# Conditioning products in longer runs, and layer 1's conditioning weights in half-size tiles that lie in the places of the partial sums

## The chip, the cores and the metric

The kernel runs on one core of a Trainium2 chip. The metric is the device time of one execution in microseconds (us), and the figure compared is the median of the runs.

## What is computed

Two transformer layers over 256 image tokens `x` and 256 context tokens `ctx`, each of width 2048. Layer 0 mixes by sliding-window attention (16 query heads, 4 key heads), layer 1 by latent attention (16 heads). Both are wrapped alike:

```
for i in range(2):
    shift, scale, gate = split(silu(c) @ ada_w[i] + ada_b[i], 3)      # the same for c_ctx
    h = rmsnorm(x, norm_g[i]) * (1 + scale) + shift                   # and hc from ctx
    o, oc = mixer_i(h, hc)                                            # projections, attention, gate, output product
    x = x + gate * o                                                  # and ctx in layer 0
```

The change touches the products `silu(c) @ ada_w[i]` for shift and scale. There are two rows (the vector `c` and the vector `c_ctx`) against a matrix of 2048 by 4096 for each layer. The gate third of `ada_w` is computed elsewhere, on VectorE, and is not touched.

## The kernel before, in words

**Wide and narrow products.** Nearly all of TensorE's work is wide: `mm3` makes a float32 product out of three fp32r products of 128 rows by 128 columns of weights, with 512 or 256 columns moving. Each weight tile of 128 x 1024 lands in a place named `raw`, ScalarE rounds it into `whi`, VectorE subtracts to get `wlo` (two places each), and TensorE uses both. The conditioning products are narrow: `sil` holds silu of both vectors, padded to 32 columns, so one product `mm_ada` uses 32 of the array's 128 columns (`tile_position=(0, 32 * j)`), in plain float32, and four of them stand side by side for j = 0 to 3. Their weights move through and need no split. A group of narrow products that is to stay together is written inside `with together(340.0)`, where 340 is what the planner adds in nanoseconds for such a group.

**Layer 0's narrow products** (`ada_first_tasks`) come in nine batches (`BATCHES`) of 1, 2 or 4 blocks of 128 outputs for shift and as many for scale. Their weights are loaded as 128 tiles of 128 x 512 (256 KB) into eight places named `k`, up to `AHEAD_K` ahead. A batch of 1 or 2 blocks cuts a tile into four pieces of 128 columns, and a batch of 4 blocks into two of 256. The products are issued as soon as four pieces are there: with every tile, or with every second one.

**Layer 1's narrow products** (`ada_rest_tasks`) are four parts of 16 tiles of 128 x 1024 (512 KB) each. Each tile lands in one of the four `raw` places, which it shares with the wide weights, and brings four products of 256 columns. They are mixed (`merge`) among the 16 gate tasks of layer 0, whose weights are `wgate`.

**Partial sums.** `atile` gives a tile of 128 x 512 in one of 24 places named `acc`. Through the input projection all 24 hold partial sums. In the last of the five groups of the projection, 16 of them are written out to DRAM (`spill`) and read back later piece by piece (`kn`, `acc`). After that the places are taken one by one by the 16 gate tiles `sg`.

**What sets the order.** Python code walks the tasks (`queue`, `step`, `pump`) and only records operations. Then `settle` replays them with a table of costs: at each turn it takes the engine that is free first and gives it the ready operation with the earliest due time. Places of a pool are given out strictly in the order in which tiles were recorded. A load is issued by SyncE (SP) as soon as its place is free and its turn has come; SP's queue is one line, so a load that waits for its place holds up those behind it. `ahead` decides how far loads and splits are recorded ahead of their use. The planner reckons a load at 2000 ns and 320 bytes a nanosecond. TensorE, too, runs its instructions strictly in the order settled here.

Of the kernel before, what the change touches and what calls it, by code (L numbers as in the profile page):

```python
# [11 lines left out]
F32 = mybir.dt.float32  # L12
# [21 lines left out]
SIDE = [0.85, 0.9, 0.8, 0.95, 1.0]  # L34
AHEAD_DMA, AHEAD_SPLIT, AHEAD_K = 0, 1, 6
LAT_T1, LAT_M1, LAT_ADA = 6.072, 6.867, 1.15
# [111 lines left out]
class Node:  # L148
    __slots__ = ("eng", "emit", "occ", "lat", "key", "n", "deps", "outs", "left", "ready", "start",
                 "end", "news", "tiles", "alt", "need", "order")  # L150

    def __init__(self, eng, emit, occ, lat, key, n):
        self.eng, self.emit, self.occ, self.lat, self.key, self.n = eng, emit, occ, lat, key, n
        self.deps, self.order, self.outs, self.news = [], [], [], []
        self.ready, self.start, self.end, self.alt = 0.0, None, None, None


SEM = 100.0
DMA_LAT, DMA_RATE = 2000.0, 320.0


class Plan:
# [57 lines left out]

    def group(self, eng, calls, occ, lat):

        real = {"PE": self.nc.tensor}[eng]
        outs, ins = [], []
        for op, args, kw in calls:
            outs.append(args[0])
            ins += [x for x in list(args[1:]) + list(kw.values()) if isinstance(x, View)]

        def emit():
            for op, args, kw in calls:  # L230
                getattr(real, op)(*[x.real() if isinstance(x, View) else x for x in args],  # L231
                                  **{n: x.real() if isinstance(x, View) else x for n, x in kw.items()})
        self.node(eng, emit, occ, lat, outs, ins)

    def node(self, eng, emit, occ, lat, outs, ins):
# [62 lines left out]
    def settle(self):  # L298
# [52 lines left out]
        for v in nodes:  # L351
            if not v.left:
                offer(v)
        out = []
        while len(out) < len(nodes):
            best = None
# [13 lines left out]
            while waiting[e] and waiting[e][0][0] <= at:  # L370
                _, _, v = heapq.heappop(waiting[e])
                heapq.heappush(able[e], (v.key, v.n, v))
            _, _, v = heapq.heappop(able[e])
            v.start = at
# [69 lines left out]
def tile_hybrid_two_layer(ctx: ExitStack, tc: tile.TileContext, a: dict):  # L444
# [71 lines left out]
    class together:  # L516


        def __init__(self, extra=0.0):
            self.extra = extra  # L520

# [3 lines left out]
        def __exit__(self, *x):  # L525
            calls = run.pop()
            occ = self.extra + sum(c[3] for c in calls)
            plan.group("PE", [c[:3] for c in calls], occ, occ + 165.0)

    def mm(ps, l, r, start, stop, share=1, **k):  # L530
        n = 1
        for d in r.shape[1:]:
            n *= d
        occ = (4 * n / 2.4 / share + (0 if share > 1 else 10) if l.dtype == F32 else max(54.0, 0.428 * n + 10))
        c = ("matmul", (ps,), dict(lhsT=l, rhs=r, start=start, stop=stop, **k), occ)
        if run:
            run[-1].append(c)
        else:
            plan.group("PE", [c[:3]], occ, occ + 165.0)
        clock[0] += (n / 2400.0 + 0.003) * (4 if l.dtype == F32 else 1) / share  # L540
# [41 lines left out]
    def ahead():  # L582
        i = head[0]
        wk = {"w": AHEAD_DMA if i >= FIRST else -1, "k": AHEAD_K}
        n = {"w": 0, "k": 0}
        for j in range(i, min(len(queue), i + 40)):
            t = queue[j]
            if t["src"] is None:
                continue
            kind = t.get("kind", "w")  # L590
            if "raw" not in t and n[kind] <= wk[kind]:
                if kind == "w":
                    t["raw"] = wp.tile([P, 1024], F32, tag="raw", name=nm("raw"))
                else:
                    t["raw"] = ktile(F32)
                SP.dma_start(t["raw"][:, :t["n"]], t["src"])
            n[kind] += 1
        n = 0
        for j in range(i, min(len(queue), i + 40)):
            t = queue[j]  # L600
            if t["src"] is None or not t["split"]:
                continue
# [139 lines left out]
    def ada_first_tasks(bi):  # L742
# [7 lines left out]
        def gen(q):  # L750
            def g(w):
# [5 lines left out]
                box["w"] += [(q * r + u, w[:, u * n:(u + 1) * n]) for u in range(r)]  # L757
                if len(box["w"]) < 4:
                    return
                with together(340.0):  # L760
                    for i, wu in box["w"]:
                        ck, j = divmod(i, ng)
                        mm_ada(box["ps"], ck, j + ng * (ck % half), wu, n, half)
# [17 lines left out]
    def ada_rest_tasks(sec, hf):  # L781
# [3 lines left out]

        def gen(ck):
            def g(w):
                if ck == 0:
                    box["ps"] = mmps()
                with together(340.0):  # L790
                    for j in range(4):
                        mm_ada(box["ps"], ck, j, w[:, j * 256:(j + 1) * 256], 256)
                yield
            return g

        for ck in range(KT):
            out.append(dict(src=a["ada1"][sec, hf, ck], n=1024, gen=gen(ck), split=False, key=None))

# [962 lines left out]
def _layout(i):  # L1761
# [22 lines left out]
    o["crow"] = C(np.concatenate([i["c"][0], i["c_ctx"]]).reshape(8, 512))  # L1784
    o["ada1"] = C(rest.reshape(2, KT, P, 2, 1024).transpose(0, 3, 1, 2, 4))

# [61 lines left out]
```

## Time and profile before

| | before |
|---|---|
| median of 3 runs (lowest to highest) | 1282.94 us (1281.44 to 1283.48) |
| the profiled execution, its time | 1277.38 us |
| its span (first to last instruction) | 1275.6 us |
| TensorE busy (PE) | 1228.1 us, 96% |
| VectorE / ScalarE busy | 930.9 us, 73% / 596.1 us, 47% |
| records of TensorE | 8252, of which 1408 belong to narrow products (two records each) |

Reading: the profiled execution is 5.6 us below the median, so a sum made against it is carried over to the median by ratio. PE counts matmuls whose ends are modelled, so starts are the better thing to measure by. "issue" in brackets is idle time in which the engine waited for nothing that the profile shows.

### The profile page before, as it was taken

The page shows a single profiled execution, that of the slowest core. Times are in us where ns is not written, and L with a number is a line of the kernel's source. Part 1 is how long each engine was busy: PE and PEld are TensorE (multiplying, and loading weights), DVE is VectorE, ACT ScalarE, POOL GpSimd, SP SyncE. Part 2 cuts the span into 40 slices and gives each one's busy share as a digit, 9 for nine tenths or more (in the row PEclk, how much of TensorE's full clock was granted, in tenths as well). Part 3 has the DMA queues.
Part 4 walks back from the last instruction along what each step waited for, and adds up shares of the span by engine and source line. Part 5 has one row for each costly group of instructions (what it writes and reads, how often), then busy time and mean ns, then how long its engine had stood idle before and what let it go on. Part 6 is the DMA issues. An engine that isn't in the chain of part 4 may idle for free.

```text
span 1275.6 us, 22429 instructions
## 1 busy us (share of the span) xinstructions
PE 1228.1 (96%) x8252; PEld 1046.5 (82%) x8252; DVE 930.9 (73%) x2260; ACT 596.1 (47%) x1434; POOL 79.7 (6%) x105
## 2 busy tenths in 40 slices
PE   3999999999999999999999999997999999999998
PEld 2777776778777777777789888986999999999998
DVE  5567687899737667667788766985588888888554
ACT  4623212222235445445565322553567777776432
POOL 0000000000100101000000000000111111110000
PEclk9999999999999999999999999998999999999999
DMA  9876797557855455455537877762343333332664
GB/s 314 306 272 201 247 337 268 190 179 278 294 206 195 145 180 188 153 186 174 194 125 232 309 267 269 263 220 80 125 137 101 115 108 108 108 113 78 201 226 141
DMA packets 96302, 249.78 MB, mean 196 GB/s; under 512 B 11328, under 2 KB 25152, under 8 KB 96192
## 3 DMA queue, kind: packets, MB, share of 16 engines
q1 hardware_dynamic: 96192, 248.35, 57.4%
q8 instruction: 64, 1.05, 0.3%
q14 instruction: 46, 0.38, 0.1%
HBM read 239.92 MB, written 8.39 MB: 195 GB/s over the span
## 4 chain that ended last, share of the span: by engine, by line
PE 80%; DVE 11%; DMA 6%; ACT 2%; issue 1%; POOL 0%; SPq 0%; DVEq 0%; ACTq 0%
PE mm L231 65%; PE tp L231 7%; DVE t L218 4%; PE tp L218 3%; DVE wlo L218 3%; PE s L231 2%; DMA t<-xT 2%; PE s L218 1%; DVE acc L218 1%; DVE h L218 1%; DMA raw<-adag 1%; ACT whi L218 1%; DMA k<-ada 1%; DMA raw<-win 1%; DVE q L218 1%
## 5 line engine op out<-in xcount | busy, mean ns | idle before, releaser
L231 PE MATMUL mm<-h,whi 128*128 128x256 f32 (+1 forms) x2368 | 536.5, 321 | 1.0 <-DVE acc L218 1.0
L218 ACT CAST whi<-raw 128x1024 fp32r<-128x1024 f32 (+3 forms) x248 | 243.8, 983 | 419.1 <-PE mm L231 254.3
L231 PEld LDWEIGHTS mm<-h,whi 128*128 128x128 f32 x2368 | 384.9, 191 | 30.7 <-issue 5.8
L218 DVE TENSOR_TENSOR wlo<-raw,whi 128x1024 fp32r<-128x1024 f32 (+3 forms) x248 | 283.0, 1142 | 156.9 <-ACT whi L218 154.9
L231 PE MATMUL mm<-h,wlo 128*128 128x256 f32 (+1 forms) x1184 | 376.8, 318 | 4.0 <-DVE wlo L218 3.7
L231 PE MATMUL mm<-whi,h 128*128 128x512 f32 (+2 forms) x1152 | 367.3, 389 | 4.1 <-ACT h L218 2.3
L231 PEld LDWEIGHTS mm<-whi,h 128*128 128x128 f32 x1152 | 216.4, 189 | 50.8 <-issue 7.5
L231 PEld LDWEIGHTS mm<-h,wlo 128*128 128x128 f32 x1184 | 225.4, 190 | 22.3 <-DVE wlo L218 7.0
L231 PE MATMUL mm<-wlo,h 128*128 128x512 f32 (+2 forms) x576 | 220.5, 383 | 10.8 <-DVE wlo L218 10.8
L231 PEld LDWEIGHTS mm<-wlo,h 128*128 128x128 f32 x576 | 109.2, 190 | 29.0 <-DVE wlo L218 12.0
L218 DVE SCALAR_TENSOR_TENSOR t<-raw,cb 128x512 f32<-128x512 f32 x112 | 72.4, 692 | 6.9 <-DMA raw<-adag 6.9
L218 DVE TENSOR_TENSOR acc<-acc,mm 128x512 f32<-128x512 f32 x96 | 62.9, 684 | 12.9 <-PE mm L231 12.7
L218 DVE TENSOR_REDUCE st<-tp 128x1 f32<-128x512 f32 (+1 forms) x76 | 45.5, 599 | 15.1 <-PE tp L231 14.9
L231 PE MATMUL mm<-pth,k 128*128 128x256 f32 x256 | 55.0, 288 | 0.0
L218 POOL TENSOR_TENSOR rr<-rr,mhalf 128x2 f32<-128x2 f32 (+2 forms) x41 | 30.2, 739 | 397.0 <-DVE rr L218 395.4
L218 ACT ACTIVATE cb<-tp,st,rq 128x512 f32<-128x512 f32 (+1 forms) x50 | 33.5, 670 | 37.4 <-DVE st L218 29.5
L218 DVE TENSOR_TENSOR ptl<-tp,pth 128x512 fp32r<-128x512 f32 x57 | 38.7, 687 | 10.3 <-ACT pth L218 10.0
L218 DVE SCALAR_TENSOR_TENSOR t<-raw,acc 128x512 f32<-128x512 f32 x64 | 42.5, 688 | 4.8 <-DMA raw<-adag 4.7
L231 PE MATMUL tp<-k,q 128*128 128x512 f32 (+1 forms) x186 | 45.9, 355 | 0.0
L218 POOL TENSOR_TENSOR rq<-rq,mhalf 128x2 f32<-128x2 f32 x32 | 26.2, 820 | 314.2 <-DVE rq L218 272.4
L231 PEld LDWEIGHTS mm<-pth,k 128*128 128x128 f32 x256 | 42.7, 188 | 1.7 <-issue 0.8
L218 ACT CAST pth<-tp 128x512 fp32r<-128x512 f32 x57 | 32.8, 585 | 24.0 <-PE tp L218 22.0
(193 smaller groups left out, 1423.1 us busy)
## 6 DMA issues: line engine op xcount, KB each, us to landing
k<-ada SPq DMA_DIRECT2D x128, 256.0 KB, 4.8
raw<-adag SPq DMA_DIRECT2D x64, 512.0 KB, 4.6
raw<-ada SPq DMA_DIRECT2D x64, 512.0 KB, 4.5
raw<-wout SPq DMA_DIRECT2D x47, 512.0 KB, 4.6
raw<-win SPq DMA_DIRECT2D x42, 512.0 KB, 4.6
raw<-mwg SPq DMA_DIRECT2D x34, 512.0 KB, 3.3
raw<-wgate SPq DMA_DIRECT2D x32, 512.0 KB, 3.8
raw<-mwo SPq DMA_DIRECT2D x29, 512.0 KB, 4.2
```

The source lines that it names most:

```text
L218: getattr(real, op)(*r, **k)
L231: getattr(real, op)(*[x.real() if isinstance(x, View) else x for x in args], **{n: x.real() if isinstance(x, View) else x for n, x in kw.i ...
```

## The change

Three things. Layer 0's narrow products are issued with every second tile (`RUN0 = 2`) whatever the width of the pieces. Layer 1's weights are laid out anew as 128 tiles of 128 x 512 (256 KB), loaded into `acc` places instead of `raw` ones, up to `AHEAD_A` ahead of the head of the queue, and issued four tiles at a time (`RUN1 = 4`), 16 products of 128 columns. The planner learns of the kind "narrow": after a narrow group on TensorE it takes another one if that is ready and due within 20 us of the first in line, and it charges the 340 ns only once for both. Besides, its cost of an fp32r product falls by 1.5 ns, and `ahead` no longer looks past a task that waits for a mark.

```diff
-AHEAD_DMA, AHEAD_SPLIT, AHEAD_K = 0, 1, 6
+AHEAD_DMA, AHEAD_SPLIT, AHEAD_K, AHEAD_A = 0, 1, 6, 3
+RUN0, RUN1 = 2, 4
...
+SWITCH, REACH = 340.0, 20.0
...
-            _, _, v = heapq.heappop(able[e])
+            v = None
+            if e == "PE" and narrow:
+                same = [x for x in able[e] if x[2].kind and x[0] < able[e][0][0] + REACH]
+                if same:
+                    x = min(same)
+                    able[e].remove(x)
+                    heapq.heapify(able[e])
+                    v = x[2]
+                    v.occ -= SWITCH
+                    v.lat -= SWITCH
+            if v is None:
+                _, _, v = heapq.heappop(able[e])
+            if e == "PE":
+                narrow = bool(v.kind)
...
-        occ = (4 * n / 2.4 / share + (0 if share > 1 else 10) if l.dtype == F32 else max(54.0, 0.428 * n + 10))
+        occ = (4 * n / 2.4 / share + (0 if share > 1 else 10) if l.dtype == F32 else max(54.0, 0.428 * n + 8.5))
...
+            if t.get("wait") and t["wait"] not in done:
+                break
...
-                    t["raw"] = ktile(F32)
+                    t["raw"] = ktile(F32) if kind == "k" else atile()
...
-                if len(box["w"]) < 4:
+                if (q + 1) % RUN0 and q < npc - 1:
                     return
-                with together(340.0):
+                with together("narrow"):
...
-        def gen(ck):
+        def gen(q):
             def g(w):
-                if ck == 0:
+                if q == 0:
                     box["ps"] = mmps()
-                with together(340.0):
-                    for j in range(4):
-                        mm_ada(box["ps"], ck, j, w[:, j * 256:(j + 1) * 256], 256)
+                    box["w"] = []
+                box["w"].append((q, w))
+                if (q + 1) % RUN1:
+                    return
+                with together("narrow"):
+                    for i, wu in box["w"]:
+                        ck, u = divmod(i, 2)
+                        for j in range(4):
+                            mm(box["ps"][32 * j:32 * j + 32, u * P:(u + 1) * P], sil[:, ck, :],
+                               wu[:, j * P:(j + 1) * P], i == 0, i == 2 * KT - 1, 4,
+                               tile_position=(0, 32 * j))
...
-            out.append(dict(src=a["ada1"][sec, hf, ck], n=1024, gen=gen(ck), split=False, key=None))
+            out.append(dict(src=a["ada1"][sec, hf, q // 2, q % 2], n=512, gen=gen(q), split=False, key=None,
+                            kind="a"))
```

Three places of the settled order show what moves. The first is TensorE's order in the gate stage of layer 0; `mm<-raw,sil` and `mm<-acc,sil` are layer 1's narrow products, all the rest is wide. Before, one tile stands alone between wide products:

```order
L231 MATMUL mm_0_282<-h_29_1129,wlo_0_259 128x512
L231 MATMUL mm_1_286<-raw_2_147,sil_91 32x256 x4
L231 MATMUL mm_0_282<-h_31_1374,whi_1_257 128x512
L231 MATMUL mm_0_282<-h_0_1384,whi_1_257 128x512
L231 MATMUL mm_0_282<-h_31_1374,wlo_1_266 128x512
```

And in the change, in the same stage:

```order
L233 MATMUL mm_0_282<-h_13_2060,wlo_1_268 128x512
L233 MATMUL mm_3_298<-acc_6_345,sil_91 32x128 x4
L233 MATMUL mm_3_298<-acc_0_290,sil_91 32x128 x4
L233 MATMUL mm_3_298<-acc_9_384,sil_91 32x128 x4
L233 MATMUL mm_3_298<-acc_10_389,sil_91 32x128 x4
L233 MATMUL mm_3_298<-acc_12_406,sil_91 32x128 x4
L233 MATMUL mm_3_298<-acc_13_413,sil_91 32x128 x4
L233 MATMUL mm_3_298<-acc_14_432,sil_91 32x128 x4
L233 MATMUL mm_3_298<-acc_3_313,sil_91 32x128 x4
L233 MATMUL mm_1_286<-pth_1_3100,k_5_2150 128x256
```

One tile of 1024 columns with four products has become a run of eight tiles of 512 columns with four products each. Over the whole program TensorE's order has 71 runs of narrow products before and 38 after: in layer 0, 25 runs of 128-column products become 18 and 10 of 256-column products become 7; in layer 1, 36 runs (17 of one tile, 10 of two, 9 of three) become 13 (4 of 12 to 16 half-size tiles, 8 of eight, 1 of four).

The second place is TensorE's start, up to the first wide product `mm<-whi,h`; `tp<-ones,q` and `tp<-t,ones` belong to the norm, `s<-k,sil` are the first batch of layer 0. Before:

```order
L231 MATMUL tp_0_199<-ones_81,q_0_159 128x1 x4
L231 MATMUL s_1_207<-k_0_125,sil_91 32x128 x4
L231 MATMUL s_1_207<-k_1_127,sil_91 32x128 x4
L231 MATMUL s_1_207<-k_2_129,sil_91 32x128 x4
L231 MATMUL s_1_207<-k_3_135,sil_91 32x128 x4
L231 MATMUL tp_2_229<-t_3_169,ones_81 128x512
L231 MATMUL s_1_207<-k_4_137,sil_91 32x128 x4
```

And in the change:

```order
L233 MATMUL tp_0_199<-ones_81,q_0_159 128x1 x4
L233 MATMUL s_1_208<-k_0_127,sil_91 32x128 x4
L233 MATMUL s_1_208<-k_1_129,sil_91 32x128 x4
L233 MATMUL tp_2_220<-t_3_169,ones_81 128x512
L233 MATMUL s_1_208<-k_2_131,sil_91 32x128 x4
L233 MATMUL s_1_208<-k_3_133,sil_91 32x128 x4
L233 MATMUL s_1_208<-k_4_139,sil_91 32x128 x4
```

Two of the batch's eight tiles have moved from ahead of the norm's product to behind it, so that six stand there where four did.

The third is SP's queue in the last group of the input projection, where finished sums are written out and weights (`win`, and `adag` for the gate third) are loaded. Before:

```order
L218 DMA raw_2_147<-win 128x1024
L218 DMA raw_1_145<-adag 128x1024
L218 DMA spill_2544<-acc_12_413 128x512
L218 DMA spill_2550<-acc_13_427 128x512
L218 DMA spill_2557<-acc_14_434 128x512
L218 DMA raw_3_149<-win 128x1024
L218 DMA spill_2573<-acc_15_441 128x512
L218 DMA raw_2_147<-adag 128x1024
L218 DMA raw_0_143<-win 128x1024
```

And in the change:

```order
L220 DMA raw_2_147<-win 128x1024
L220 DMA spill_2544<-acc_12_406 128x512
L220 DMA spill_2552<-acc_13_413 128x512
L220 DMA raw_3_149<-adag 128x1024
L220 DMA spill_2572<-acc_14_432 128x512
L220 DMA acc_12_406<-ada 128x512
L220 DMA spill_2576<-acc_15_435 128x512
L220 DMA acc_13_413<-ada 128x512
L220 DMA raw_1_145<-win 128x1024
L220 DMA acc_14_432<-ada 128x512
L220 DMA raw_2_147<-adag 128x1024
L220 DMA acc_15_435<-ada 128x512
```

Each `acc<-ada` load goes into the place that a spill has just been sent from, and waits until that spill has landed; the next `win` load now stands behind two of them and behind a fourth spill. Apart from the narrow products the same instructions stand in both programs; some of the wide ones change places with each other, mostly in the gate stage and in layer 1's attention.

## Rows read from the trace of the kernel before

**Rows 1.** The page, busy time, share of the span and instructions of each engine.

```profile
PE 1228.1 (96%) x8252; PEld 1046.5 (82%) x8252; DVE 930.9 (73%) x2260; ACT 596.1 (47%) x1434; POOL 79.7 (6%) x105
```

**Rows 2.** Windows of 40 us: busy time and instructions of each engine, PEclk, DMA share, GB/s.

```profile
0.00:40.00 40.00, 19.03 (x174) 13.95 (x175) 17.54 (x37) 20.47 (x35) 1.22 (x5) 0.96 0.89 300
40.00:80.00 40.00, 39.64 (x323) 30.23 (x322) 26.78 (x65) 16.94 (x28) 1.53 (x7) 1.00 0.89 311
...
280.00:320.00 40.00, 40.00 (x181) 33.08 (x180) 38.20 (x99) 10.47 (x22) 1.50 (x2) 1.00 0.78 265
...
480.00:520.00 40.00, 40.00 (x253) 30.62 (x252) 29.55 (x92) 21.79 (x61) 4.02 (x5) 1.00 0.49 168
...
680.00:720.00 40.00, 39.40 (x309) 38.20 (x309) 31.94 (x63) 16.85 (x23) 0.00 (x0) 1.00 0.86 285
```

**Rows 3.** Timeline of PE around two runs of layer 1: start, us, engine, line, operation, count.

```profile
347.32 0.39 PE L231 MATMUL mm<-h,whi 128*128 128x512 f32 x1
347.55 0.39 PE L231 MATMUL mm<-h,wlo 128*128 128x512 f32 x1
347.86 0.64 PE L231 MATMUL mm<-raw,sil 128*32 128x256 f32 x8
348.43 0.50 PE L231 MATMUL mm<-h,whi 128*128 128x512 f32 x1
...
386.61 0.39 PE L231 MATMUL mm<-h,wlo 128*128 128x512 f32 x1
386.92 1.50 PE L231 MATMUL mm<-raw,sil 128*32 128x256 f32 x24
388.36 0.50 PE L231 MATMUL mm<-h,whi 128*128 128x512 f32 x1
```

**Rows 4.** Timeline of PE around a run of layer 0 with 128-column products.

```profile
73.35 0.39 PE L231 MATMUL mm<-whi,h 128*128 128x512 f32 x1
73.67 1.52 PE L231 MATMUL s<-k,sil 128*32 128x128 f32 x48
75.11 0.50 PE L231 MATMUL mm<-whi,h 128*128 128x512 f32 x1
```

**Rows 5.** Timeline of PE at the start; in brackets idle time and what ended it.

```profile
19.69 1.93 PE L231 MATMUL s<-k,sil 128*32 128x128 f32 x32
21.93 2.05 PE L231 MATMUL tp<-t,ones 128*128 128x512 f32 x2 [0.30 <-DVE t L218]
23.91 1.59 PE L231 MATMUL s<-k,sil 128*32 128x128 f32 x32
...
28.89 0.79 PE L231 MATMUL mm<-whi,h 128*128 128x512 f32 x1 [2.25 <-ACT h L218]
```

**Rows 6.** Timeline of SP's queue in the last group of the projection.

```profile
308.20 1.85 SPq L218 DMA_DIRECT2D spill<-acc  x3
310.95 0.33 SPq L218 DMA_DIRECT2D raw<-win  x1
311.55 0.32 SPq L218 DMA_DIRECT2D spill<-acc  x1
```

**Rows 7.** Timeline of ACT, the same stretch.

```profile
316.15 1.05 ACT L218 CAST whi<-raw 128x1024 fp32r<-128x1024 f32 x1 [6.12 <-DMA raw<-win]
...
319.86 1.05 ACT L218 CAST whi<-raw 128x1024 fp32r<-128x1024 f32 x1 [1.93 <-PE mm L231]
```

**Rows 8.** Timeline of DVE, the same stretch.

```profile
317.24 1.23 DVE L218 TENSOR_TENSOR wlo<-raw,whi 128x1024 fp32r<-128x1024 f32 x1 [0.29 <-ACT whi L218]
```

**Rows 9.** DMA issues: count, KB each, median us from issue to landing.

```profile
k<-ada SPq DMA_DIRECT2D x128, 256.0 KB, 4.8
...
raw<-ada SPq DMA_DIRECT2D x64, 512.0 KB, 4.5
...
spill<-acc SPq DMA_DIRECT2D x16, 256.0 KB, 3.2
```

**Rows 10.** Waits of PE from 200 to 240 us: us in total, times, longest.

```profile
PE s L231 <- DMA k<-ada: 3.0, 3, 1.6
```

More of the change, by code (lines that the diff above doesn't have):

```diff
@@ L149 @@
     __slots__ = ("eng", "emit", "occ", "lat", "key", "n", "deps", "outs", "left", "ready", "start",
-                 "end", "news", "tiles", "alt", "need", "order")
+                 "end", "news", "tiles", "order", "kind")
     def __init__(self, eng, emit, occ, lat, key, n):
@@ L154, in __init__ @@
         self.deps, self.order, self.outs, self.news = [], [], [], []
-        self.ready, self.start, self.end, self.alt = 0.0, None, None, None
+        self.ready, self.start, self.end, self.kind = 0.0, None, None, None
 SEM = 100.0
+SWITCH, REACH = 340.0, 20.0
 DMA_LAT, DMA_RATE = 2000.0, 320.0
@@ L219, in add, with group @@
         self.node(eng, emit, occ, lat, outs, ins)
-    def group(self, eng, calls, occ, lat):
+    def group(self, eng, calls, occ, lat, kind=None):
         real = {"PE": self.nc.tensor}[eng]
@@ L233, in group @@
         self.node(eng, emit, occ, lat, outs, ins)
+        self.nodes[-1].kind = kind
     def node(self, eng, emit, occ, lat, outs, ins):
@@ L354, in settle @@
         out = []
+        narrow = False
         while len(out) < len(nodes):
@@ L516, in tile_hybrid_two_layer, with __init__ @@
     class together:
-        def __init__(self, extra=0.0):
-            self.extra = extra
+        def __init__(self, kind=None):
+            self.kind, self.extra = kind, SWITCH if kind else 0.0
         def __enter__(self):
@@ L527, in __exit__ @@
             occ = self.extra + sum(c[3] for c in calls)
-            plan.group("PE", [c[:3] for c in calls], occ, occ + 165.0)
+            plan.group("PE", [c[:3] for c in calls], occ, occ + 165.0, self.kind)
     def mm(ps, l, r, start, stop, share=1, **k):
@@ L583, in ahead @@
         i = head[0]
-        wk = {"w": AHEAD_DMA if i >= FIRST else -1, "k": AHEAD_K}
-        n = {"w": 0, "k": 0}
+        wk = {"w": AHEAD_DMA if i >= FIRST else -1, "k": AHEAD_K, "a": AHEAD_A}
+        n = {"w": 0, "k": 0, "a": 0}
         for j in range(i, min(len(queue), i + 40)):
             t = queue[j]
+            if t.get("wait") and t["wait"] not in done:
+                break
             if t["src"] is None:
@@ L600, in ahead @@
             t = queue[j]
+            if t.get("wait") and t["wait"] not in done:
+                break
             if t["src"] is None or not t["split"]:
@@ L784, in ada_rest_tasks @@
         out = []
-        def gen(ck):
+        def gen(q):
             def g(w):
-                if ck == 0:
+                if q == 0:
                     box["ps"] = mmps()
-                with together(340.0):
-                    for j in range(4):
-                        mm_ada(box["ps"], ck, j, w[:, j * 256:(j + 1) * 256], 256)
+                    box["w"] = []
[9 more added lines that the diff above has]
+                               tile_position=(0, 32 * j))
+                box["w"] = []
                 yield
             return g
-        for ck in range(KT):
-            out.append(dict(src=a["ada1"][sec, hf, ck], n=1024, gen=gen(ck), split=False, key=None))
+        for q in range(2 * KT):
+            out.append(dict(src=a["ada1"][sec, hf, q // 2, q % 2], n=512, gen=gen(q), split=False, key=None,
+                            kind="a"))
         def fin():
@@ L1784, in _layout @@
     o["crow"] = C(np.concatenate([i["c"][0], i["c_ctx"]]).reshape(8, 512))
-    o["ada1"] = C(rest.reshape(2, KT, P, 2, 1024).transpose(0, 3, 1, 2, 4))
+    o["ada1"] = C(rest.reshape(2, KT, P, 2, 4, 2, P).transpose(0, 3, 1, 5, 2, 4, 6).reshape(2, 2, KT, 2, P, 512))
     w = i["swa_w_in"][0]
```

## The prediction

> **What bounds the kernel now.** Start with the busy line: TensorE 96%, VectorE 73%, ScalarE 47% [rows 1]. A share over the whole span hides stages, so read the windows next [rows 2]. After the first 40 us, in which TensorE is busy for only 19.03, it is busy for 39.40 to 40.00 of every 40 us shown. In the gate stage (480 to 520) it is busy 40.00 of 40 while VectorE has 29.55 and the DMA engines 0.49. Only in the projection's last group (280 to 320) does a second engine come near, VectorE with 38.20. So a nanosecond less on TensorE is a nanosecond off the time as long as nothing else is late. But busy is modelled: what a narrow run really costs must be read from starts.
>
> **What a run costs.** Two wide products of 512 columns start 0.23 us apart (347.32 and 347.55) [rows 3]. Between 347.55 and 348.43 stands one narrow tile: 0.88, less the 0.23 of the wide product, is 0.65 us. Between 386.61 and 388.36 stand three: 1.75 less 0.23 is 1.52. Two more tiles thus cost 0.87, or 0.435 each, and 0.65 - 0.435 = 0.215 is left, which a run pays once, however long it is: the way into the narrow products and out again. Layer 0 has the same price: six tiles (48 records) cost 75.11 - 73.35 - 0.23 = 1.53 [rows 4]; at half of 0.435 for 128 columns that is 6 x 0.2175 = 1.305 and 0.225 over. Rows are rounded to 0.01, so I take 0.225.
>
> **The sum, part by part.**
>
> *Runs that vanish.* The order has 71 runs before and 38 after, 33 fewer: 33 x 0.225 = 7.4 us less. Ten are in layer 0, 23 in layer 1. The planner's 340 ns is not used here; it is a figure of its table.
>
> *The products themselves.* Before, 64 tiles at 0.435 = 27.8 us; now 128 at 0.2175 = 27.8. No difference (a rounding of 0.0025 in each tile would be 0.3 us).
>
> *Start.* The first wide product starts at 28.89 after a wait for ScalarE's `h` [rows 5]. That waits, through the norm's factors, for the first batch, whose last four tiles run from 23.91 in 1.59 us behind the norm's product at 21.93. In the change six stand there. Two more tiles cost 2 x 0.2175 = 0.44 at the price of [rows 4], or 2 x 1.93 / 4 = 0.97 at that of the first four (19.69); the mean clock of the first 40 us is 0.96 and not 1.00 [rows 2], so part of it runs at the lower level. I take 0.7 us more, nearer to the 1.59 / 4 = 0.40 a tile of the same place. The idle time before 21.93 gives nothing back, for that product waits for VectorE.
>
> *The projection's last group.* Loads into `acc` wait for the spill out of that place. Before, three spills go out from 308.20 and a `win` load follows at 310.95 [rows 6]. It lands at 316.15, when the rounding that had waited 6.12 us for it starts [rows 7], and VectorE's part ends at 317.24 + 1.23 = 318.47 [rows 8]. TensorE leaves the tile before it at about 319.86, when the next rounding gets its place [rows 7]: 1.4 us to spare. In the change that load stands behind a load that waits for the second spill. Sent at about 308.8 (1.85 / 3 apart), it lands 3.2 later [rows 9], at 312.0; so `win` goes out about 1.1 later, and 2 x 256 KB more are ahead of it. At 265 / 0.78 = 340 GB/s [rows 2] those are 1.5 us. 2.6 late less 1.4 to spare leaves TensorE standing for 1.2 us. Behind the blocked load wait the `win` and `adag` loads, and behind those VectorE, which has 1.8 us to spare in this window. There are four batches of spills, of which three are followed by `win` loads: at least 0, if the other places have more to spare, at most 3.6. I take 1.2.
>
> *Long runs and their last tile.* TensorE stands if a tile of a run has not landed. Before, this happened once to a run, the one of ten tiles between 200 and 240 us: 3.0 us [rows 10]; that run stays as it is. The first run of layer 1 has 16 tiles, the last of which are loaded behind the last spills, so it is the likeliest to wait: 0 to 3.0 us, and I take 0.5. Layer 0's four runs of eight tiles are in the same danger and within the same bound: those of six [rows 4] did not wait.
>
> *At nothing.* The freed `raw` places let `wgate` come earlier, but TensorE waited for none of it (40.00 of 40). A run of 16 tiles holds up attention for 16 x 0.2175 = 3.5 us; VectorE has 10 us to spare in a window there, and wide products always stand ready behind it. Were that cover gone, at most one such 3.5 would show. Stopping `ahead` at a mark changes when loads are recorded, not the order of places.
>
> Sum: -7.4 + 0 + 0.7 + 1.2 + 0.5 = -5.0. The profiled execution took 1277.38, so 1272.4; by ratio to the median of 1282.94 (x 1.00435) that is 1277.9 us. With the terms at their best it is -7.4 + 0.44 = -7.0, or 1275.9; at their worst -7.4 + 0.3 + 0.97 + 3.6 + 3.0 = +0.5, or 1283.4.
>
> **A rule against it.** Layer 1's weights now come in 128 loads of 256 KB instead of 64 of 512 KB. In the trace, 40 to 80 us, where tiles of 256 KB are part of the stream, 311 GB/s go at a DMA share of 0.89, that is 349 GB/s for a full share; 680 to 720 has 285 at 0.86, that is 331 [rows 2], and the conditioning loads land in 4.8 us at 256 KB and in 4.5 at 512 KB, medians [rows 9]. Small loads overlap, and cost no more share by the byte. If they did not overlap, 128 x 4.8 = 614 us would stand against 64 x 4.5 = 288, and 326 more would make 1609; I give that less than 0.01, within the slower case below. The Trainium skill says otherwise (DMA: Bandwidth & Descriptors, section Bandwidth): loads should be batched to 1 MiB or more, and its fit gives each a fixed 2.0 us besides its bytes at 436 GB/s. By that, as an estimate from the page, one load after another would take 128 x 2.6 = 333 us against 64 x 3.2 = 205, 128 us more. The trace does not bear that out: 349 GB/s for a full share leaves no room for a fixed 2.0 us in each load.
>
> **Rivals.**
>
> *The loads eat the gain (0.22).* The group at 280 to 320 has VectorE at 38.20 of 40 and loads that already landed too late for ScalarE (6.12). If all three places stall and the first long run waits its 3.0, little is left: between 1280.4 and 1283.4, say 1282. Against it: TensorE itself stood for none of these in that window, 40.00.
>
> *The planner's order gets better (0.15).* Its cost of a 512-column product, 0.428 x 512 + 8.5 = 228 ns, now meets the 0.23 of [rows 3]; before it was 229, so the drift is small, but wide work changes places everywhere. TensorE is idle for 1275.6 - 1228.1 = 47.5 us, 21 of them at the start. A tenth of the other 26.5 would be 2.7 less, on top of the best terms: -9.7, or 1273.2. Nothing in the profile points to it.
>
> *The long runs wait, and it is slower (0.10).* The planner counts 2.0 us and 320 bytes a nanosecond for a load, 2.8 us for 256 KB, where the trace has 4.8 [rows 9]. A place is refilled only when the run before it has let go, and TensorE can do nothing else while it stands in a run. With 7.4 - 0.7 = 6.7 to lose over layer 1's 13 runs, 0.52 us a run takes the gain, and 0.71 makes it slower by 0.2%. At 1 us each it is 13 - 6.7 = +6.3, or 1289. For it: the wait of [rows 10] is just this. Against it: the DMA engines are half idle there (0.49), and eight tiles at 0.77 each are loaded in 6.2 us, while layer 1's 13 runs share the whole gate stage.
>
> *The change doesn't do what it says*, if the price were by product and not by run: then nothing is gained and the loads still cost, 1283 to 1285. One and three tiles at 0.65 and 1.52 [rows 3] exclude it but for the mixture with the first rival, where its chance lies.
>
> **The numbers.** My forecast has 0.53, at 1277.9 (own range 1275.9 to 1280.4). Three runs of this kernel differ by 0.16%, so about 0.2% (2.6 us) is what can be told from no change. Faster is below 1280.4: 0.53 + 0.15 = 0.68; within 0.2%: 0.22; slower: 0.10. The range from 1273.2 to 1283.4 leaves out the slower case and the tail of the better order, under 2 in 10.
>
> **What would show it.** Right: 38 narrow runs; about 0.225 left over in each; TensorE's records of a run of eight tiles at 0.225 + 8 x 0.2175 = 1.97 us between the wide starts; the first wide product at about 29.6; the last layer 1 run ending some 5 us earlier; the layers after it as long as before. Wrong: waits of TensorE for `acc<-ada` within layer 1's runs; waits for `wlo` between 290 and 350 of more than 4 us together; new waits in the out product or in layer 1's attention, where nothing is meant to change.

## The result, and the profile after

| | before | after |
|---|---|---|
| median (lowest to highest) of 4 runs each | 1282.19 us (1281.01 to 1283.48) | 1266.80 us (1265.24 to 1268.16) |
| the profiled execution, its time | 1277.38 us | 1265.24 us |
| narrow runs in the order | 71 | 38 |

The ratio is 0.9879, 95% interval 0.9862 to 0.9897: 15.4 us faster, where 5 were forecast, and below the range (1273.2 to 1283.4). First the lines that answer to [rows 1] and [rows 2]: the busy line of the page after, and windows of 40 us (busy time and instructions of PE, PEld, DVE, ACT, POOL, then PEclk, DMA share, GB/s).

```profile
PE 1219.3 (97%) x8764; PEld 1065.6 (84%) x8764; DVE 930.7 (74%) x2260; ACT 593.9 (47%) x1434; POOL 80.5 (6%) x105
```

```profile
0.00:40.00 40.00, 18.77 (x170) 13.50 (x171) 17.42 (x37) 19.75 (x33) 1.22 (x5) 0.96 0.85 291
40.00:80.00 40.00, 40.00 (x329) 31.29 (x328) 26.54 (x65) 17.37 (x29) 3.93 (x7) 1.00 0.91 326
...
280.00:320.00 40.00, 39.94 (x180) 32.51 (x178) 36.81 (x96) 10.65 (x22) 2.19 (x3) 1.00 0.85 309
480.00:520.00 40.00, 40.00 (x333) 33.22 (x331) 30.70 (x94) 22.41 (x63) 3.02 (x4) 1.00 0.37 119
...
680.00:720.00 40.00, 39.89 (x270) 36.90 (x269) 30.03 (x62) 13.84 (x18) 0.00 (x0) 1.00 0.91 313
```

TensorE is about as busy as before in each of these windows (40.00 of 40 in the gate stage). Busy shares do not show this gain, for the time of a switch between narrow and wide products is counted as busy. Starts show it. The timeline of PE after, around a run of layer 1 (12 half-size tiles, 96 records), answers to [rows 3]:

```profile
383.29 0.39 PE L233 MATMUL mm<-h,wlo 128*128 128x512 f32 x1
383.61 2.83 PE L233 MATMUL mm<-acc,sil 128*32 128x128 f32 x96
386.37 0.73 PE L233 MATMUL mm<-h,whi 128*128 128x512 f32 x2
386.94 0.39 PE L233 MATMUL mm<-h,wlo 128*128 128x512 f32 x1
387.17 0.62 PE L233 MATMUL mm<-h,whi 128*128 128x512 f32 x2
387.63 0.39 PE L233 MATMUL mm<-h,wlo 128*128 128x512 f32 x1
```

From 383.29 to 386.37 it is 3.08; less 0.23 and 12 x 0.2185 that leaves 0.23, the price forecast. (0.2185 for a half-size tile is the finer figure from after: runs of 16, 32 and 48 records, which are two, four and six tiles, take 0.44 more for each two tiles.) But the reader should go two rows on. The two wide products right behind the run take 386.94 - 386.37 = 0.57, the next two of the same kind 387.63 - 387.17 = 0.46. The second wide product behind a run starts **0.11 late**. Layer 0 has the same, answering to [rows 4], on PE's timeline:

```profile
72.68 0.39 PE L233 MATMUL mm<-whi,h 128*128 128x512 f32 x1
73.00 1.08 PE L233 MATMUL s<-k,sil 128*32 128x128 f32 x32
74.01 0.50 PE L233 MATMUL mm<-whi,h 128*128 128x512 f32 x1
74.34 0.40 PE L233 MATMUL mm<-wlo,h 128*128 128x512 f32 x1
74.58 0.62 PE L233 MATMUL mm<-whi,h 128*128 128x512 f32 x2
```

74.01 - 72.68 - 0.23 - 4 x 0.2185 = 0.23, and then 0.33 from 74.01 to 74.34 where 0.24 follows. Over all runs in front of 512-column products the spacing behind the first one has a median of 0.337 us, 0.227 elsewhere, in both kernels (54 of the 71 runs before and 31 of the 38 after stand in front of such products). A run of this kind therefore costs 0.229 + 0.110 = 0.339 us, half as much again as I took. A sign stood in the rows of before: the first wide product behind a run has 0.50, not 0.39, in [rows 3] and [rows 4].

The start, answering to [rows 5], on PE's timeline:

```profile
19.30 1.08 PE L233 MATMUL s<-k,sil 128*32 128x128 f32 x16
21.53 2.04 PE L233 MATMUL tp<-t,ones 128*128 128x512 f32 x2 [1.16 <-DVE t L220]
23.51 2.79 PE L233 MATMUL s<-k,sil 128*32 128x128 f32 x48
...
29.49 0.69 PE L233 MATMUL mm<-whi,h 128*128 128x512 f32 x1 [2.11 <-ACT h L220]
```

Six tiles stand behind the norm's product; the first wide product comes at 29.49, 0.60 later than before (0.7 forecast). Counted from the norm's product it comes 1.0 later (7.96 us behind it for 6.96 in [rows 5]); the norm's product itself came 0.40 earlier in this execution.

The last group of the projection, answering to [rows 6] and [rows 7]: SP's queue, then ACT.

```profile
306.40 1.33 SPq L220 DMA_DIRECT2D spill<-acc  x2
...
311.70 0.44 SPq L220 DMA_DIRECT2D raw<-win  x1
```

```profile
317.26 1.04 ACT L220 CAST whi<-raw 128x1024 fp32r<-128x1024 f32 x1
```

The `win` load goes out 5.3 us behind the first spill, 2.75 before. The delay is there and larger than forecast, but the rounding at 317.26 has no wait in brackets: the weights were early enough. VectorE has 36.81 in the window from 280 to 320 (38.20 before), TensorE 39.94, and the profile lists no wait of TensorE from 280 to 640 us. The loads, answering to [rows 9], the waits of PE from 200 to 240 us, answering to [rows 10], and the group of layer 1's narrow products (busy, mean ns, idle time before it):

```profile
k<-ada SPq DMA_DIRECT2D x128, 256.0 KB, 4.6
...
acc<-ada SPq DMA_DIRECT2D x128, 256.0 KB, 4.8
...
spill<-acc SPq DMA_DIRECT2D x16, 256.0 KB, 4.4
```

```profile
PE s L233 <- DMA k<-ada: 3.0, 3, 1.4
```

```profile
L233 PE MATMUL mm<-acc,sil 128*32 128x128 f32 x1024 | 30.6, 274 | 0.0
```

TensorE never stood for a half-size tile (0.0); the only wait for conditioning weights is the old one in the run of ten. The Trainium skill's rule to batch loads to 1 MiB or more (DMA: Bandwidth & Descriptors, section Bandwidth) would speak against halving the loads; the trace does not bear that out, for TensorE waited for none of them, and they land in 4.8 us at 256 KB where those of 512 KB took 4.5. The fit behind the prediction's estimate of 128 us stands on that page of the Trainium skill in the section Anatomy of one DMA — SWDGE (gpsimd) path, so it was measured on loads that GpSimd issues; the loads here are issued by SyncE, and none of the 128 us shows.

**What the profile pair hides.** Two executions differ by TensorE's clock too. Behind the run of ten, in which it stands for 3.0 us, it fell to the lower level (1.2 GHz) in the profiled execution of after (granted clock 0.50 from 211.5 to 216.0 us) and not in that of before. The window 200 to 240 us, of before, of after, and of the experiment e6_one:

```profile
200.00:240.00 40.00, 37.03 (x274) 28.07 (x273) 33.54 (x87) 9.09 (x14) 0.00 (x0) 1.00 0.71 239
```

```profile
200.00:240.00 40.00, 37.01 (x260) 29.20 (x259) 34.56 (x89) 10.39 (x16) 0.00 (x0) 0.91 0.59 205
```

```profile
200.00:240.00 40.00, 36.48 (x257) 29.31 (x256) 37.34 (x94) 11.13 (x18) 0.00 (x0) 1.00 0.61 196
```

At 0.91 it loses at most 0.09 x 40 = 3.6 us. Over the fourteen kernels profiled here this window has 0.91 in four, 0.96 in seven and 1.00 in three. Whole executions differ too. In 62 of the kernel before (61 beside the experiments, and the profiled one), the nine with a mean clock of 0.995 took 1280.3 on average, the ten with 0.992 took 1283.7. The profile of before had 0.995 and is the quickest of all; that of after had 0.993. That may be part of why the profiles differ by 12.1 and the medians by 15.4.

### The profile page after: what moved, and what is told of

Same layout as the page of the kernel before. It is cut to its first block, busy times and chain, and to the rows that moved or that the text cites. A ratio compares the mean times of both kernels' runs of the same rounds, so it can differ in the third digit from the quotient of the medians.

```text
span 1263.5 us, 23603 instructions
## 1 busy us (share of the span) xinstructions
PE 1219.3 (97%) x8764; PEld 1065.6 (84%) x8764; DVE 930.7 (74%) x2260; ACT 593.9 (47%) x1434; POOL 80.5 (6%) x105
## 4 chain that ended last, share of the span: by engine, by line
PE 85%; DVE 8%; DMA 4%; issue 2%; ACT 1%; POOL 0%; SPq 0%; DVEq 0%; ACTq 0%
PE mm L233 71%; PE tp L233 7%; DVE t L220 3%; PE tp L220 3%; PE s L233 2%; DVE wlo L220 2%; PE s L220 1%; DVE acc L220 1%; DMA raw<-adag 1%; DMA t<-xT 1%; DVE h L220 1%; ACT whi L220 1%; DMA h<-xT 0%; DMA q<-xT 0%; DMA raw<-wout 0%
## 5 line engine op out<-in xcount | busy, mean ns | idle before, releaser
L233 PEld LDWEIGHTS mm<-wlo,h 128*128 128x128 f32 x576 | 109.8, 191 | 30.6 <-DVE wlo L220 13.2
L220 POOL TENSOR_TENSOR rq<-rq,mhalf 128x2 f32<-128x2 f32 x32 | 23.4, 733 | 318.1 <-DVE rq L220 296.4
```

What stands on the lines that cost most here:

```text
L220: getattr(real, op)(*r, **k)
```

## Experiments

All ratios are to runs of the kernel before on the same chip; "runs" in the table are narrow runs in TensorE's order. One hundredth is 12.8 us. The diffs are against the changed kernel.

| kernel | layer 1's weights | runs | median us | ratio (95% interval) |
|---|---|---|---|---|
| after | acc, by four | 38 | 1266.80 | 0.9879 (0.9862 to 0.9897) |
| e1_places | acc, by one | 78 | 1286.23 | 1.0032 (1.0014 to 1.0049) |
| e2_raw | raw | 42 | 1271.56 | 0.9916 (0.9895 to 0.9937) |
| e3_planner | raw | 70 | 1281.15 | 0.9999 (0.9988 to 1.0010) |
| e4_cost10 | acc, by four | 38 | 1265.84 | 0.9876 (0.9859 to 0.9894) |
| e5_nopick | acc, by four | 53 | 1272.48 | 0.9919 (0.9896 to 0.9942) |
| e6_one | acc, by one | 40 | 1266.37 | 0.9879 (0.9857 to 0.9900) |
| e7_pairs | acc, by two | 69 | 1278.31 | 0.9967 (0.9955 to 0.9979) |
| e8_long0 | acc, by four | 36 | 1266.86 | 0.9880 (0.9859 to 0.9900) |
| e9_raw69 | raw | 69 | 1280.36 | 0.9977 (0.9962 to 0.9992) |
| e10_singles | acc, by one | 77 | 1283.68 | 1.0003 (0.9989 to 1.0016) |
| e11_raw3 | acc, by four | 36 | 1291.06 | 1.0059 (1.0045 to 1.0073) |
| e12_lone | acc, by four | 103 | 1303.54 | 1.0171 (1.0142 to 1.0200) |

### The parts of the change, one at a time

The first four were made with the prediction's price in mind. e1_places: of the change only the half-size tiles in `acc` (to the changed kernel: layer 0's old condition, one tile at a time, no taking, cost 10, no stop at a mark).

```diff
-RUN0, RUN1 = 2, 4
+RUN0, RUN1 = 2, 1
...
-            if e == "PE" and narrow:
+            if False:
...
-                if (q + 1) % RUN0 and q < npc - 1:
+                if len(box["w"]) < 4:
...
-max(54.0, 0.428 * n + 8.5))
+max(54.0, 0.428 * n + 10))
...
-            if t.get("wait") and t["wait"] not in done:
-                break
...
```

> Only layer 1's weights change: half-size tiles in the acc places, issued one by one, no taking of a second narrow group, the planner's costs as before. The order has 78 narrow runs where before has 71. Theory: a run costs 0.229 us on TensorE wherever its weights lie, and the places themselves do little: +1.6 us for 7 more runs, less at most 3 us for the waits of 640 to 760 us that the changed kernel no longer has, so between 1280.5 and 1284 beside 1282.2 of before. Rival, the raw places that come free are the gain that the runs do not explain (15.4 - 7.6 = 7.8 us): 1282.2 + 1.6 - 7.8 = 1276.

Measured: 1.0032, 4.1 us slower (1.8 to 6.3). The rival that the freed places give the rest falls. The theory's range, up to 1284, is missed too: 7 more runs should have cost 1.6 and the vanished waits given something back. At 0.339 the runs come to 2.4; what else is lost here stays open.

e2_raw: the changed kernel with layer 1's tiles, layout and places of before.

```diff
...
-            out.append(dict(src=a["ada1"][sec, hf, q // 2, q % 2], n=512, gen=gen(q), split=False, key=None,
-                            kind="a"))
+            out.append(dict(src=a["ada1"][sec, hf, ck], n=1024, gen=gen(ck), split=False, key=None))
...
```

> The change without the acc places: layer 1's weights are 1024 wide in raw places as before, everything else as in the changed kernel. 42 narrow runs, 29 fewer than before. Theory: -29 x 0.229 = -6.6 us, so 1275.6 if the places hold all the rest of the gain; if the rest lies in the planner's cost and order, it stays, and the time is that of the changed kernel and four runs more, 1266.8 + 0.9 = 1267.7. The rival that only the places count has 1282.

Measured: 0.9916, 10.8 us for 29 runs, where 6.6 were expected. None of the three numbers on record fits; 0.339 a run gives 9.8. Its long runs wait once for a tile of 512 KB in `raw`, which never happens to the tiles in `acc`; PE's waits from 330 to 360 us:

```profile
PE mm L233 <- DMA raw<-ada: 1.7, 1, 1.7
```

e3_planner: the changed planner's cost and the stop at a mark alone; tiles, places and runs as before.

```diff
-            if e == "PE" and narrow:
+            if False:
...
-                if (q + 1) % RUN0 and q < npc - 1:
+                if len(box["w"]) < 4:
...
-            out.append(dict(src=a["ada1"][sec, hf, q // 2, q % 2], n=512, gen=gen(q), split=False, key=None,
-                            kind="a"))
+            out.append(dict(src=a["ada1"][sec, hf, ck], n=1024, gen=gen(ck), split=False, key=None))
...
```

> Only the planner's cost of a 512-column product (8.5 for 10) and the stop of ahead at a mark, no taking together, tiles and places as before. 70 narrow runs. Theory: -0.2 us for one run, 1282. Rival, the new order is the part that the runs do not explain: 1282.2 - 7.8 = 1274.4.

Measured: 0.9999. The planner's new cost with the stop at a mark gives nothing by itself.

e4_cost10: the changed kernel with cost 10.

```diff
-max(54.0, 0.428 * n + 8.5))
+max(54.0, 0.428 * n + 10))
```

> The changed kernel with the planner's old cost (10). 38 narrow runs as in the change, but the run of ten tiles between 200 and 240 us, behind which TensorE's granted clock fell to 0.50 in the changed kernel, is not in this order. Theory of runs: 1266.8, less up to 3 us if that fall belongs to the wait in the ten-tile run (1263.8). Rival, the new cost gives the part that the runs do not explain: 1266.8 + 7.8 = 1274.6.

Measured: 0.9876, the same as the change. The cost is not where the gain lies, from this side either. Breaking up the run of ten gave nothing that can be told.

### The price of a run

Now the 0.110 behind the run was found. e5_nopick takes only the taking of a second group out of the changed kernel:

```diff
-            if e == "PE" and narrow:
+            if False:
```

> The changed kernel without the taking of a second narrow group: tiles, places and costs as in the change, 53 narrow runs for 38. New theory, a run costs 0.339 us: 0.229 up to the start of the wide product behind it and 0.110 more up to the start of the one after that: +5.1 us on the 1266.2 that the changed kernel and its twin with cost 10 show, 1271.3. The price of the prediction, 0.225 to 0.229: +3.4, 1269.6. Rival, only the places of the weights count and the runs cost nothing: 1266.2.

Measured: 0.9919, 5.1 us more than the change for 15 runs. The interval (some 3.7 us either way) holds both prices, and not the rival in which runs cost nothing.

e6_one keeps the taking but hands layer 1's tiles over one by one, and layer 0's as before:

```diff
-RUN0, RUN1 = 2, 4
+RUN0, RUN1 = 2, 1
...
-                if (q + 1) % RUN0 and q < npc - 1:
+                if len(box["w"]) < 4:
```

> Layer 1's tiles handed over one by one and layer 0's as before, but a second narrow group is taken behind a first: 40 narrow runs, where the kernel with the acc places and no taking had 78 and 1286.2 us. Places are the same in both. New theory: -38 x 0.339 = -12.9, so 1273.3, or lower by some us if the small waits go with the runs. The price of the prediction: -38 x 0.229 = -8.7, 1277.5.

Measured: 0.9879, as fast as the change with 40 runs and without either grouping by hand: of the three ways to fewer runs, the taking alone is enough. It is 6.9 us faster than the 1273.3 expected; that base (e1_places) carried other costs, so e10_singles was made to match it.

e7_pairs: the changed kernel without the taking and in pairs of tiles.

```diff
-RUN0, RUN1 = 2, 4
+RUN0, RUN1 = 2, 2
...
-            if e == "PE" and narrow:
+            if False:
```

> The changed kernel without the taking and with layer 1 in runs of two tiles of 512 columns: acc places, new costs, layer 0 in pairs of loaded tiles, but 69 narrow runs, nearly the 71 of before. New theory: 31 runs more than the change, +10.5 us on 1266.2, so 1276.7. The price of the prediction: +7.1, 1273.3. If the runs were no more than a part and the freed places were worth 4 us by themselves: 1281.5 - 0.7 - 4 = 1276.8 by that count too, so this kernel checks that the two add up, and the one with 53 runs tells the price.

Measured: 0.9967. To the change it is 31 runs and 11.3 us: 0.36 a run; 7.1 us lies outside (about 2.7 either way).

e10_singles: e6_one without the taking.

```diff
-            if e == "PE" and narrow:
+            if False:
```

> The kernel with layer 1 tile by tile in acc places, no taking and layer 0 as before (78 runs, 1.0032 of before), but with the new costs and the stop at a mark: 77 runs. Theory (0.339 us a run, places worth 4 us): +2.0 - 4 = 1280. Rival, tiles handed over one by one lose what the places give, whatever the costs: 1.0032 - 0.0003 = 1285.7.

Measured: 1.0003, 1283.7 us, between the two numbers. Beside e1_places only the cost, the stop at a mark and one run differ, and that is 3.7 us (some 2.8 either way), though e3_planner and e4_cost10 show nothing of the kind. And three pairs now differ by the taking alone: e10_singles and e6_one, 37 runs and 15.9 us; e9_raw69 (below) and e2_raw, 27 and 7.8; e5_nopick and the change, 15 and 5.1. Together 79 runs and 28.8 us, 0.36 a run; with the intervals' half-widths added in squares (6.0 us), 0.29 to 0.44. The 0.225 of the prediction is outside, 0.339 inside. The taking also changes the order around the runs, so these pairs weigh a run with whatever goes with it.

e12_lone weighs the price by itself, with 64 narrow tiles added to the gate stage:

```diff
                     mm3(ps[:, :n], wh[:, us], wl[:, us], hh, hl, kt == 0, kt == KT - 1)
+                    if n == NT and u % 4 == 1:
+                        lone = together()
+                        lone.extra = SWITCH
+                        e = sps()
+                        with lone:
+                            for j in range(4):
+                                mm(e[32 * j:32 * j + 32, :P], sil[:, kt, :], f(hh[:, j * P:(j + 1) * P]),
+                                   True, True, 4, tile_position=(0, 32 * j))
                     yield
```

> The changed kernel with 64 lone narrow tiles of 128 columns more (four products each, of `sil` with a resident tile, into a place that nobody reads) among layer 0's gate products, four to a gate tile: work that the change does not have, to weigh the price by itself. 103 narrow runs for 38. The added products cost 64 x 0.2185 = 14.0 us by either theory. New theory, 0.339 a run: 65 x 0.339 = 22.0, together +36.0, 1302. The price of the prediction, 0.229: 65 x 0.229 = 14.9, together +28.9, 1295. In the trace: the wide product behind each lone tile 0.229 + 0.2185 later than without it, and the next one another 0.110 later (new theory) or 0.00 later.

Measured: 1.0171, which is 37.4 us above the change (some 4.3 either way): 36.0 fits, 28.9 does not. In its trace, the timeline of PE and then of PEld (weight loads) around one of the lone tiles:

```profile
516.38 0.39 PE L233 MATMUL mm<-h,wlo 128*128 128x512 f32 x1
516.70 0.43 PE L233 MATMUL tp<-h,sil 128*32 128x128 f32 x8
517.05 0.73 PE L233 MATMUL mm<-h,whi 128*128 128x512 f32 x2
517.62 0.39 PE L233 MATMUL mm<-h,wlo 128*128 128x512 f32 x1
517.85 0.62 PE L233 MATMUL mm<-h,whi 128*128 128x512 f32 x2
518.31 0.40 PE L233 MATMUL mm<-h,wlo 128*128 128x512 f32 x1
```

```profile
516.15 0.19 PEld L233 LDWEIGHTS mm<-h,wlo 128*128 128x128 f32 x1
516.69 0.16 PEld L233 LDWEIGHTS tp<-h,sil 128*32 128x32 f32 x8 [0.35 <-issue]
517.05 0.30 PEld L233 LDWEIGHTS mm<-h,whi 128*128 128x128 f32 x2 [0.20 <-issue]
517.39 0.19 PEld L233 LDWEIGHTS mm<-h,wlo 128*128 128x128 f32 x1
```

517.05 - 516.38 - 0.23 - 0.22 = 0.22, and 0.57 against 0.46 for the two products behind. The loads show where it sits: in the stream a weight load starts 0.23 ahead of its product (516.15 for the product of 516.38). Behind the run the first load starts with its product, at 517.05, and the second only 0.30 - 0.19 = 0.11 after it; the second product again follows its load by 0.23, and so it is 0.11 late. After that the loads are ahead again.

The narrow products differ from the wide ones in two things: they fill 32 columns for 128 (four of them side by side), and they are plain float32 where the others are fp32r. Which of the two costs the time can be read in the kernel before, where a product of the norm, `s<-t,ones`, is plain float32 at full width and stands between fp32r products, on PE's timeline:

```profile
854.43 0.40 PE L231 MATMUL mm<-whi,h 128*128 128x512 f32 x1
854.67 0.59 PE L231 MATMUL s<-t,ones 128*128 128x256 f32 x2
854.91 0.58 PE L231 MATMUL mm<-whi,h 128*128 128x512 f32 x1
855.33 0.40 PE L231 MATMUL mm<-wlo,h 128*128 128x512 f32 x1
```

From 854.43 to 855.33 it is 0.90; less two wide products (0.45) and 0.435 for the 256 columns, 0.01 is left. So the number format costs nothing that can be told, and the 0.339 belongs to the change between 128 and 32 columns. A long first record (0.58) and a late second product (0.42 behind the first) stand here too, but the first product came just as much too early: only the sum up to the old rhythm tells a loss.

### What the runs leave over

33 x 0.339 is 11.2 of the 15.4 us, or 10.8 if each run is priced by what stands behind it (0.110 in front of 512 columns, 0.103 in front of 256, 0.056 in front of transpositions). e9_raw69 is the partner of e7_pairs with layer 1's tiles and places of before (the edit of e2_raw) and no taking.

```diff
-            if e == "PE" and narrow:
+            if False:
...
-            out.append(dict(src=a["ada1"][sec, hf, q // 2, q % 2], n=512, gen=gen(q), split=False, key=None,
-                            kind="a"))
+            out.append(dict(src=a["ada1"][sec, hf, ck], n=1024, gen=gen(ck), split=False, key=None))
...
```

> Layer 1's weights 1024 wide in raw places, no taking of a second group, layer 0 in pairs of loaded tiles and the new costs: 69 narrow runs, just as many as the kernel with pairs of half-size tiles in the acc places, which took 0.9967 of before. Only the places and sizes of layer 1's weights differ between the two. Theory that now stands (runs at 0.339 us, and the acc places worth some 4 us by themselves): 2 runs less than before, 0.9995, 1281.3 beside 1282 of before. Rival, the 4 us come from layer 0's pairs or from the costs: 0.9967, 1277.8.

Measured: 0.9977, between the two. At 69 runs each, `acc` places are worth 1.3 us (some 2.5 either way), not 4. Against e3_planner, layer 0's pairs are worth 2.8, of which one run is 0.3, with as wide an interval.

e11_raw3: three `raw` places for four.

```diff
-                    t["raw"] = wp.tile([P, 1024], F32, tag="raw", name=nm("raw"))
+                    t["raw"] = wp.tile([P, 1024], F32, tag="raw", name=nm("raw"), bufs=3)
```

> The changed kernel with three raw places for four in the whole program: 36 narrow runs. Theory, the acc places help because the wide weights then have all four raw places to themselves: taking one away gives the 4 us back, or more, since the projections and the out product lose the place too: 1270.5 or above, with longer waits for wlo. Rival, the fourth raw place does nothing and the gain lies elsewhere: 1266.2 - 0.7 = 1265.5.

Measured: 1.0059. The theory's number was met (1270.5 or above), and its reason was not. The waits of PE, in the whole span and then from 330 to 640 us, where layer 1's tiles used to share `raw`:

```profile
PE mm L233 <- DVE wlo L220: 27.1, 29, 8.6
```

```profile
PE mm L233 <- DVE wlo L220: 0.6, 1, 0.6
```

In the whole span PE waits 27.1 for `wlo` (13.2 in the change), but only 0.6 of it lies where the change frees the place. There three places are enough as far as TensorE is concerned; 6.1 of the waits lie between 240 and 330 us and 6.2 between 660 and 830, in the projection and behind the gate stage.

e8_long0, a try at a faster version: layer 0 by four tiles.

```diff
-AHEAD_DMA, AHEAD_SPLIT, AHEAD_K, AHEAD_A = 0, 1, 6, 3
-RUN0, RUN1 = 2, 4
+AHEAD_DMA, AHEAD_SPLIT, AHEAD_K, AHEAD_A = 0, 1, 7, 3
+RUN0, RUN1 = 4, 4
...
-max(54.0, 0.428 * n + 8.5))
+max(54.0, 0.428 * n + 10))
```

> The changed kernel with layer 0 in runs of four loaded tiles, one more k tile ahead, and the planner's old cost 10: 36 narrow runs, and again four tiles of the first batch ahead of the norm's product. New theory: 2 runs less, -0.7, and the start some 0.7 us earlier: 1264.8 beside 1266.2. Rival, the longer runs of layer 0 wait for their tiles (loads of k land in 4.6 us): above 1266.2.

Measured: 0.9880, no gain. I misread the start: all eight tiles now stand behind the norm's product, as PE's timeline shows (64 records), so the earlier start that was expected did not come:

```profile
23.81 3.23 PE L233 MATMUL s<-k,sil 128*32 128x128 f32 x64
```

No version is clearly faster than the change.

## Why the prediction was wrong

**What a run costs: the step that failed.** The count (71 to 38) and the mechanism (a price once a run, whatever its length) were right. The size was not: I ended the measurement at the start of the first wide product, but the one behind that is late too. 0.225 was really 0.339, so the term is -11.2 (-10.8 by what stands behind each run), not -7.4. Shown in three ways: the spacing of starts, the kernels that differ by the taking alone (0.29 to 0.44), and the lone tiles (37.4, where 36.0 and 28.9 stood against each other).

**The products themselves**: 0, as forecast; both traces give 0.2185 for 128 columns.

**Start**: +0.6 for +0.7, in part by luck. The six tiles took 2.79 us where four took 1.59, which is 1.2 more and above the 0.97 given as the worst, and the first wide product came 1.0 later behind the norm's; that product came 0.4 earlier, which the prediction did not count on.

**The projection's last group**: 0 for +1.2. The queueing was right, the slack was not: I took the spare time from one chain of before (1.4 us) and let the rest fall on TensorE, though it had waited for nothing there.

**Long runs and their last tile**: 0 for +0.5 in `acc`. The danger is real in `raw`: e2_raw waits 1.7 us once.

**At nothing**: `wgate` is right (0.6 us even with three places). That order and places outside the runs are worth nothing at all is not borne out. Of the 10.4 us by which the forecast was too small, the price of a run makes 3.4 to 3.8, the projection 1.2 and the long runs 0.5; some 5 us stay open. Layer 0's pairs (about 2.5) and the `acc` places (about 1.3) would make up most of them, but neither stands clear of its own interval by much, if at all. The planner's new cost gives nothing in e3_planner and e4_cost10, but some of the 3.7 us between e1_places and e10_singles may be its. TensorE's idle time falls from 47.5 to 1263.5 - 1219.3 = 44.2 us.

The profiles show where it falls. The prediction said that layer 1's last run would end some 5 us earlier and that the layers behind it would take as long as before. The last run of before and that of after, on PE's timeline:

```profile
645.16 1.07 PE L231 MATMUL mm<-raw,sil 128*32 128x256 f32 x16
```

```profile
634.24 1.96 PE L233 MATMUL mm<-acc,sil 128*32 128x128 f32 x64
```

It ends some 10 us earlier, and the other 2 of the 12.1 come behind it, where only the order of wide work changed. The waits of PE from 640 to 760 us, before and after:

```profile
PE mm L231 <- DVE wlo L218: 1.3, 3, 0.6
PE mm L231 <- DVE acc L218: 1.0, 1, 1.0
PE s L231 <- ACT cb L218: 0.7, 1, 0.7
```

```profile
PE mm L233 <- DVE wlo L220: 0.2, 1, 0.2
```

They fall from 3.0 to 0.2 us. That is not the `acc` places alone, for e2_raw, with layer 1's tiles in `raw`, has 0.5 there and e10_singles, with them in `acc`, 2.1; and e4_cost10, as fast as the change, still has 1.6. What makes them go is not settled. Nor is it settled why tiles handed over one by one without the taking lose what the places give (e1_places, e10_singles).

**By ratio to the median**: this took the profile of before, the quickest execution seen, as a fair sample of how profile and median stand. After's profile lies 1.6 us under its median, not 5.6. Nothing in one profile could tell that. It has no part in the miss, for the forecast gain is 5.0 us with the ratio or without.

**Rivals**: the loads that eat the gain, the long runs that wait, and the change without effect are all excluded by the measured time. The better order (1273.2, with 0.15) came nearest, though the largest known part of what was missing is the price and not the order; how much of the open 5 us is order was not weighed by itself.

## What to carry to other kernels

Measure what an interruption costs up to the point where the rhythm is the old one again, not up to the next start: a first record that is longer than its neighbours (0.50 for 0.39) says that the one behind it is late, and only the sum says whether time was lost (0.339 behind narrow products, 0.01 around the norm's wide one). Where a planner can choose, as here, letting it take a second group of the same kind while one is running can be worth more than grouping by hand: the taking alone leaves 40 runs of 77 (1266.4 us), the grouping alone 53 (1272.5 us). And a stall that a queue will produce is worth nothing until the engine at its end has been seen to wait.

## What the runs showed of the hardware

Changing from 128-column to 32-column products and back costs TensorE 0.229 us up to the first wide product, and 0.110 more for the one behind it (0.103 where both have 256 columns, 0.056 for transpositions of 128), whatever the length of the run. A plain float32 product of full width between fp32r products costs 0.01 besides its own time. The Trainium skill says that changing the tiling mode drains TensorE (TensorEngine Tiling (Array Packing), Key Properties); the trace agrees with a fixed loss for each pair of changes, 0.339 us, and puts 0.110 of it behind the first wide product, where the weight loads are not yet ahead again.

Behind waits of about 3 us in a narrow run, the granted clock falls to the lower level in some profiled executions and not in others: e3_planner waits 3.6 us and has a PEclk of 0.91 in the window from 200 to 240 us, e6_one waits 3.5 and has 1.00. These are different programs; with one and the same, the kernel before, the mean clock of an execution goes from 0.989 to 0.997.
